# Attention heads: the order of score tiles, transposes and low parts on TensorE and VectorE

## The chip, the cores and the metric

The kernel runs on one core of one Trainium2 chip. The metric is the device time of one execution in microseconds (us); the figure for a kernel is the median of its runs.

## What is computed

Two sequences of 512 tokens with 1024 features go through a trunk of two layers: Fourier mixing and a squared-ReLU MLP, then grouped-query attention and a second MLP. The change touches the attention heads only. There are 8 query heads and 2 key/value heads of 128 features for each sequence, so 16 heads in all:

```python
q = axial_rope(rms_norm(q, q_gain)) * (HEAD_DIM ** -0.5)
k = axial_rope(rms_norm(k, k_gain))
s = jnp.einsum("bqkgd,bskd->bkgqs", q_blk, k)
p = jax.nn.softmax(s, axis=-1)
o = jnp.einsum("bkgqs,bskd->bqkgd", p, v)
```

Everything is in 32-bit floats. A product is made of three passes over operands that are split into a high part (rounded to the short format that TensorE takes at full rate) and a low part (the rest).

## The kernel before

The kernel is one straight program of Tile code: the instructions of each engine are ordered by a scheduler at compile time, except inside a `manual_schedule` block, where the named engines keep the order of the source. Every engine runs its own list in order and waits by semaphores.

One helper makes every three-pass product: `mm3`, lines 81 (high by high), 82 (the moving operand's low part) and 83 (the stationary operand's low part). `split` takes a tile apart: line 86 is a ScalarE cast that makes the high part, line 87 a VectorE subtraction that makes the low part. `behind(x, y)` tells the scheduler that x must stand after y on their engine.

The heads loop runs over n = 1 to 16. In turn n it makes the scores of head n and finishes head n - 1. These names are used below, all for one turn:

- **S0 to S3**, the four score tiles (`scores`, line 1510): 128 queries by 512 keys each, one `mm3` of three 512-column matmuls. After each: a row maximum on VectorE (line 1512), an exponential on ScalarE that also sums (line 1514, two records: the activation and the reading of the sum), a reciprocal on VectorE (line 1515) and a scaling on GpSimd (line 1516), which leaves the probabilities p0 to p3 of head n.
- **T0 to T3**, the transposes of head n - 1's probabilities (`transpose_p`, line 1522): four 128-column transposes each, one out of each of p0 to p3 of the turn before. Each is followed by a split out of PSUM: a cast (line 86) and a low part (line 87).
- **Q**, the transposes of head n + 1's query (`transpose_q`, line 1501), four of them, and a split.
- **V**, the product of the values with the transposed probabilities (`values`, line 1531): four `mm3` groups, one for each of T0 to T3, so twelve 512-column matmuls. The first matmul of group i takes the high part of Ti, the second its low part. After it a ScalarE copy (line 1538) and, for the eight heads of the first sequence, a split as well (line 1541).

In the source a turn is S0, T0, S1, T1, S2, T2, S3, T3, Q, V. No engine has a manual order in this loop: the scheduler sets it. Two other streams run through the loop. In turns 3 to 7 the last query rows are normalised and rotated (`todo`, lines 155 to 160, 1467, 1475, 1478, 1480). From turn 7 on the first weights of the output projection are loaded and split (`first_rows`; line 86 and 87 on tiles named w); the `fresh` lines put such a low part behind the last low part and the last reciprocal of a turn.

The PSUM pool has eight buffers of one bank, the pool of the probabilities eight tiles.

Of the kernel before, what the change touches and what calls it, by code (L numbers as in the profile page):

```python
# [16 lines left out]
ALU = mybir.AluOpType  # L17
AX = mybir.AxisListType
# [5 lines left out]
NT = S // P  # L24
# [20 lines left out]
def trunk_kernel(ctx, tc, x_in, xt_in, y_out, tables, rope, gfour, gcol, grow, gfin,  # L45
                 w_four, w_nyq, w_qkv, w_o, w_a22, w_up, w_row2, w_row4, w_sum2, w_sum4, w_down):
    nc = tc.nc
# [17 lines left out]
    def slot(shape, dt):  # L65
        return act.tile(shape, dt, tag="u4", name=nm("u"))

    def tm(shape=(P, 512), dt=F32):
        return tmp.tile(list(shape), dt, tag="t2", name=nm("t"))

    def small(n=4):
        return sm.tile([P, n], F32, tag="s", name=nm("s"), padded_shape=[P, 8])

    def ps():
        return psp.tile([P, 512], F32, tag="ps", name=nm("ps"))

    def f32(ap):
        return ap.bitcast(F32)

    def mm3(out, lh, ll, rh, rl, first, last):  # L80
        nc.tensor.matmul(out, lh, rh, start=first, stop=False)  # L81
        nc.tensor.matmul(out, lh, rl, start=False, stop=False)  # L82
        nc.tensor.matmul(out, ll, rh, start=False, stop=last)  # L83

    def split(dst_hi, dst_lo, src, eng=nc.vector):
        hi = nc.scalar.copy(dst_hi, src)  # L86
        return hi, eng.tensor_sub(dst_lo, src, f32(dst_hi))  # L87

    def behind(x, y, sync=False):

        kind = mybir.DependencyClass.Sync if sync else mybir.DependencyClass.NoSync
        tc.add_manual_dep(x.ins, y.ins.name, mybir.DependencyInfo(kind, mybir.DependencyReason.SCHED_ONLY),
                          reason="order")
# [5 lines left out]
    def load_raw(src, shape=(P, 1024)):  # L99
        raw = rawp.tile(list(shape), F32, tag="raw", name=nm("raw"))  # L100
        nc.sync.dma_start(raw, src)
        return raw
# [618 lines left out]
    ET = mybir.EngineType  # L721
# [714 lines left out]
    def head_squares(raw, h0, n, ss, scale=1.0):  # L1436
        junk = tm((P, n * HD), BF16)
        for h in range(h0, h0 + n):
            nc.scalar.activation(junk[:, (h - h0) * HD : (h - h0 + 1) * HD], raw[:, h * HD : (h + 1) * HD],
                                 AF.Square, scale=scale, accum_out=ss[:, h : h + 1])  # L1440
# [41 lines left out]
            yield  # L1482

    vt, kr, kT, qr = {}, {}, {}, {}
    heads_out, ahead, fresh, last_made = Blocks(None), [], [], []

    def transpose_k(q):
        for h in range(NKV):
# [8 lines left out]
    def transpose_q(q, h):  # L1497
        pt = ps()
        c = (h % 2) * HD
        for t in range(NT):  # L1500
            nc.tensor.transpose(pt[:, t * P : (t + 1) * P], qr[q, h // 2][:, t, c : c + HD], ident)  # L1501
        qT = slot([P, 2, 512], F32R)
        split(qT[:, 0], qT[:, 1], pt)
        return qT

    def scores(q, h, qT, t):
        kk = kT[q, h // 4]
        s = ps()
        cols = slice(t * P, (t + 1) * P)
        mm3(s, qT[:, 0, cols], qT[:, 1, cols], kk[:, 0], kk[:, 1], True, True)  # L1510
        m, sm_ = small(1), small(1)
        nc.vector.tensor_reduce(m[:, :1], s, AX.X, ALU.max, negate=True)
        p = tm()
        last_made[:] = [nc.scalar.activation(p, s, AF.Exp, bias=m[:, :1], accum_out=sm_[:, :1]),
                        nc.vector.reciprocal(sm_[:, :1], sm_[:, :1])]
        nc.gpsimd.tensor_scalar(p, p, sm_[:, :1], 1.0, ALU.mult, ALU.mult)
        return p

    def transpose_p(probs, sc):
        pt = ps()  # L1520
        for t in range(NT):
            nc.tensor.transpose(pt[:, t * P : (t + 1) * P], probs[t][:, sc * P : (sc + 1) * P], ident)  # L1522
        k = slot([P, 2, 512], F32R)
        return k, split(k[:, 0], k[:, 1], pt)

    def values(q, h, pts):
        o = ps()
        c = (h // 4) * HD
        for sc in range(NT):
            vh, vl = vt[q][0][:, sc, c : c + HD], vt[q][1][:, sc, c : c + HD]  # L1530
            mm3(o, vh, vl, pts[sc][:, 0], pts[sc][:, 1], sc == 0, sc == NT - 1)
        i, j = h // 2, h % 2
        name = "b11" if h < 4 else "b21"
        if j == 0:
# [99 lines left out]
    def tile_qkv(cg, q, t):  # L1634
        if (cg, q, t) in transposes:
            transpose_k(transposes[cg, q, t])
        if (cg, q) == (2, 0):
            o = qkv(cg, q, t, ws[cg], KC - 2, KC, begun[t])
        else:
            o = qkv(cg, q, t, ws[cg])  # L1640
        if (cg, q, t) == (2, 0, 0):
            token_scale(1)
        r = rs[q][:, t : t + 1]
        if cg == 2:
            split_scaled(vt[q][0][:, t], vt[q][1][:, t], o[:, 256:], r)
            return norm_rope(o, NKV, rt["k"], [t], [kr[q][:, t]], scale=r)
        outs = [qr[q, 2 * cg + i][:, t] for i in range(2)]
        if (cg, q, t) != (1, 1, 1):
            return norm_rope(o, 4, rt["q"], [t], outs, scale=r)
        raw = slot([P, 512], F32)  # L1650
        nc.scalar.activation(raw, o, AF.Copy, scale=r)
        return norm_rope(raw, 4, rt["q"], [t], outs)


    with tc.manual_schedule(engines={ET.Activation, ET.DVE}):
        for cg in (2, 0, 1):
            later = next_ws({2: 0, 0: 1}[cg]) if cg != 1 else iter(())
            for q in range(NSEQ):
# [26 lines left out]
    heads = [(q, h) for q in range(NSEQ) for h in range(NH)]  # L1685
    raw, ss = slot([P, 1024], F32), small(8)
    with tc.manual_schedule(engines={ET.Activation}):
        o = qkv(1, 1, 2, ws[1])
        tc.keep_in_program_order(nc.scalar.preload_act_table_set("natural_log_exp_and_others"))
        probs = [scores(*heads[0], first, t) for t in range(NT)]  # L1690
        nc.scalar.activation(raw[:, :512], o, AF.Copy, scale=rs[1][:, 2:3])
        qT = transpose_q(*heads[1])
        for _ in turned:
# [4 lines left out]
    todo = norm_rope(raw, 4, rt["q"], [2, 3], [qr[1, 2 + i][:, t] for t in (2, 3) for i in range(2)],  # L1698
                     ss, 2, nc.gpsimd)
    assert next(keeping, 0) == 0  # L1700
    first_rows = (None for _ in range(4) for _ in load_kept())
    for n in range(1, len(heads) + 1):
        pts, nxt = [], []
        for t in range(NT):
            if n < len(heads):
                nxt.append(scores(*heads[n], qT, t))
            k, both = transpose_p(probs, t)
            pts.append(k)
            if t == NT - 1 and fresh:
                for a, b, c in zip(fresh.pop(), both, last_made):  # L1710
                    behind(a, b)
                    if nxt:
                        behind(a, c)
            if n > 2 and t == 0:
                for _ in range(3 if n == 3 else 1):
                    next(todo, None)
        last = nxt[-1] if nxt else last
        if n + 1 < len(heads):
            qT = transpose_q(*heads[n + 1])
        values(*heads[n - 1], pts)  # L1720
        if n == 2:
            head_squares(raw, 4, 4, ss)
        probs = nxt
        if n > 6:
            next(first_rows, None)

    blocks = Blocks(2 * KC)
    behind(nc.scalar.activation(one[:, :1], last[:, :1], AF.Sqrt), both[0])
# [1 line left out]
    todo, e, rows = heads_out.plain_sums(), [tm() for _ in range(4)], []  # L1730
# [80 lines left out]
    for f in range(2 * PLAIN):  # L1811
        raw = load_raw(plain[f], (P, 2, 512))
# [60 lines left out]
    with tc.manual_schedule(engines={ET.PE, ET.Activation, ET.DVE, ET.Pool, ET.SP}):  # L1873
# [17 lines left out]
        x, z = xtok  # L1891
# [58 lines left out]
        for i in range(2):  # L1950
            a, b = slice(i * 256, i * 256 + 256), slice(512 + i * 256, 768 + i * 256)
# [158 lines left out]
```

## Time and profile before

| | |
|---|---|
| median of 3 runs | 1675.03 us (1674.89 to 1676.52) |
| the profiled execution's own time | 1675.69 us |
| its span, first to last instruction | 1673.9 us |
| PE busy | 1662.0 us (99%) |
| DVE (VectorE) busy | 1263.5 us (75%) |
| ACT (ScalarE) busy | 871.5 us (52%) |
| POOL (GpSimd) busy | 392.5 us (23%) |
| heads loop, first S0 to last V, by TensorE's rows | 843.06 to 964.64 us of the span |

In the rows of the profile PE is TensorE, PEld its weight loads, DVE VectorE, ACT ScalarE, POOL GpSimd. Matmuls are pipelined, so that a matmul's row is longer than the distance to the next one; what TensorE needs is read from the distance between starts. The same holds for DVE and ACT, whose records overlap a little when they stand back to back. A row of a timeline gives start, duration, engine, line, operation, output and input, the count of merged instructions, and in brackets the idle time before it and who ended it.

### The profile page before, as it was taken

The page shows a single profiled execution, that of the slowest core. Times are in us where ns is not written, and L with a number is a line of the kernel's source. Part 1 is how long each engine was busy: PE and PEld are TensorE (multiplying, and loading weights), DVE is VectorE, ACT ScalarE, POOL GpSimd, SP SyncE. Part 2 cuts the span into 40 slices and gives each one's busy share as a digit, 9 for nine tenths or more (in the row PEclk, how much of TensorE's full clock was granted, in tenths as well). Part 3 has the DMA queues.
Part 4 walks back from the last instruction along what each step waited for, and adds up shares of the span by engine and source line. Part 5 has one row for each costly group of instructions (what it writes and reads, how often), then busy time and mean ns, then how long its engine had stood idle before and what let it go on. Part 6 is the DMA issues. An engine that isn't in the chain of part 4 may idle for free.

```text
span 1673.9 us, 22285 instructions
## 1 busy us (share of the span) xinstructions
PE 1662.0 (99%) x7845; PEld 1387.2 (83%) x7845; DVE 1263.5 (75%) x1848; ACT 871.5 (52%) x1539; POOL 392.5 (23%) x364
## 2 busy tenths in 40 slices
PE   9999999999999999999999999999999999999998
PEld 8988888888888888888888888888888888888887
DVE  8879776557886869869888877777854487978865
ACT  6766444446342435447688855554554552433334
POOL 3321443221000001325454303004422220000002
PEclk9999999999999999999999999999999999999999
DMA  9843655449775757425501146334544696757522
GB/s 310 264 152 110 210 184 188 152 168 370 253 228 165 247 172 233 163 83 198 168 1 39 63 177 226 114 120 169 209 147 167 225 373 192 228 157 248 167 101 101
DMA packets 122321, 303.00 MB, mean 181 GB/s; under 512 B 12217, under 2 KB 13881, under 8 KB 122209
## 3 DMA queue, kind: packets, MB, share of 16 engines
q1 hardware_dynamic: 98848, 254.18, 43.8%
q0 software_dynamic: 8960, 21.05, 6.0%
q10 hardware_dynamic: 14400, 26.35, 4.2%
q8 instruction: 61, 1.00, 0.2%
q14 instruction: 52, 0.42, 0.1%
HBM read 218.11 MB, written 82.38 MB: 180 GB/s over the span
## 4 chain that ended last, share of the span: by engine, by line
PE 95%; DVE 2%; DMA 1%; ACT 1%; issue 1%; POOL 0%; SPq 0%; DVEq 0%; POOLq 0%; ACTq 0%
PE ps L927 74%; PE ps L83 6%; PE ps L81 6%; PE ps L82 6%; PE ps L1522 2%; DMA u<-x 0%; DMA u<-w_four 0%; PE ps L1501 0%; DMA raw<-w_up 0%; PE ps L191 0%; PE ps L496 0%; PE ps L493 0%; DVE w L87 0%; DVE u L715 0%; DVE raw L977 0%
## 5 line engine op out<-in xcount | busy, mean ns | idle before, releaser
L927 PE MATMUL ps<-u,w 128*128 128x512 f32 x4944 | 1131.0, 389 | 0.0
L927 PEld LDWEIGHTS ps<-u,w 128*128 128x128 f32 x4944 | 926.5, 188 | 194.9 <-ACT u L960 1.7
L86 ACT CAST w<-raw 128x1024 fp32r<-128x1024 f32 (+1 forms) x216 | 213.7, 994 | 308.4 <-PE ps L927 234.7
L87 DVE TENSOR_TENSOR w<-raw,w 128x1024 fp32r<-128x1024 f32 (+1 forms) x216 | 251.3, 1167 | 75.5 <-ACT w L86 75.3
L86 ACT CAST u<-u 128x1024 fp32r<-128x1024 f32 x144 | 145.0, 1047 | 87.0 <-PE ps L927 37.8
L87 DVE TENSOR_TENSOR u<-u,u 128x1024 fp32r<-128x1024 f32 x144 | 173.4, 1232 | 18.7 <-ACT u L86 17.8
L927 PE MATMUL ps<-u,u 128*128 128x512 f32 x600 | 143.2, 389 | 0.3 <-DVE t L1014 0.3
L1164 POOL DMA_DIRECT2D raw<-w_sum x32 | 27.7, 866 | 468.3 <-DMA raw<-w_sum 207.1
L1137 DVE TENSOR_TENSOR u<-ps,u 128x512 f32<-128x512 f32 x160 | 109.3, 685 | 37.1 <-PE ps L927 34.5
L1045 POOL TENSOR_TENSOR u<-u 128x512 f32<-128x512 f32 x28 | 37.6, 1343 | 425.0 <-ACT u L942 425.0
L927 PEld LDWEIGHTS ps<-u,u 128*128 128x128 f32 x600 | 112.5, 188 | 24.4 <-DVE t L1014 0.7
L81 PE MATMUL ps<-u,u 128*128 128x512 f32 (+2 forms) x340 | 128.7, 381 | 0.0
L83 PE MATMUL ps<-u,u 128*128 128x512 f32 (+2 forms) x340 | 124.0, 366 | 0.1
L82 PE MATMUL ps<-u,u 128*128 128x512 f32 (+2 forms) x340 | 123.6, 364 | 0.0
L182 POOL TENSOR_TENSOR t<-t,t 128x512 f32<-128x512 f32 (+1 forms) x54 | 79.3, 1472 | 188.1 <-ACT t L178 187.2
L941 ACT ACTIVATE t<-t 128x512 f32<-128x512 f32 x64 | 40.5, 632 | 109.9 <-DVE t L1014 96.4
L83 PEld LDWEIGHTS ps<-u,u 128*128 128x128 f32 x340 | 64.2, 189 | 11.0 <-DVE u L468 0.5
L87 DVE TENSOR_TENSOR u<-ps,u 128x512 fp32r<-128x512 f32 (+3 forms) x112 | 68.0, 634 | 5.5 <-ACT u L86 4.9
L82 PEld LDWEIGHTS ps<-u,u 128*128 128x128 f32 x340 | 64.4, 189 | 8.4 <-DVE u L87 0.3
L81 PEld LDWEIGHTS ps<-u,u 128*128 128x128 f32 x340 | 64.4, 189 | 7.8
L1001 DVE TENSOR_TENSOR t<-ps,u 128x512 f32<-128x512 f32 x32 | 22.0, 687 | 59.9 <-PE ps L927 52.0
L86 ACT CAST u<-ps 128x512 fp32r<-128x512 f32 (+3 forms) x112 | 59.4, 557 | 8.1 <-PE ps L1522 6.1
(266 smaller groups left out, 2012.4 us busy)
## 6 DMA issues: line engine op xcount, KB each, us to landing
raw<-w_up SPq DMA_DIRECT2D x80, 512.0 KB, 4.6
u<-spill_t SPq DMA_DIRECT2D x60, 512.0 KB, 6.9
raw<-w_sum SPq DMA_DIRECT2D x56, 512.0 KB, 5.8
u<-spill_b SPq DMA_DIRECT2D x45, 512.0 KB, 6.3
spill_t<-u SPq DMA_DIRECT2D x84, 256.0 KB, 2.0
spill_b<-t ACTq DMA_DIRECT2D x60, 256.0 KB, 4.4
raw<-w_row SPq DMA_DIRECT2D x28, 512.0 KB, 5.1
park<-u SPq DMA_DIRECT2D x24, 512.0 KB, 4.8
```

The lines of the kernel that those rows point to most:

```text
L81: nc.tensor.matmul(out, lh, rh, start=first, stop=False)
L82: nc.tensor.matmul(out, lh, rl, start=False, stop=False)
L83: nc.tensor.matmul(out, ll, rh, start=False, stop=last)
L86: hi = nc.scalar.copy(dst_hi, src)
L87: return hi, eng.tensor_sub(dst_lo, src, f32(dst_hi))
L182: nc.gpsimd.tensor_add(acc[q][:, :n], acc[q][:, :n], s[:, :n])
L927: nc.tensor.matmul(o, w[x][:, sl], h[k][y], start=first and k + i == 0, stop=k == n - 1 and i == 2, skip_group_check=not first)
L941: nc.scalar.activation(t, src, AF.Relu)
L1045: eng.tensor_sub(t[:, 0], b12, b11)
L1137: return nc.vector.tensor_add(x, o, x)
L1164: nc.gpsimd.dma_start(s[:, 1], w[:, 3], accum_op=ALU.add)
L1522: nc.tensor.transpose(pt[:, t * P : (t + 1) * P], probs[t][:, sc * P : (sc + 1) * P], ident)
```

## The change

The loop is put into a `manual_schedule` block for TensorE, so its order there is that of the source. The source order becomes S0, S1, T0, T1, Q, S2, S3, T2, T3, V: scores and transposes come in pairs, and Q follows T1 instead of T3. The maximum of S2 is put behind two low parts on VectorE, that of T1 and that of Q. The orders of VectorE, ScalarE and GpSimd are still the scheduler's. No instruction is added or removed.

```diff
     def transpose_q(q, h):
...
-        split(qT[:, 0], qT[:, 1], pt)
+        q_low[:] = split(qT[:, 0], qT[:, 1], pt)[1:]
         return qT
...
-        nc.vector.tensor_reduce(m[:, :1], s, AX.X, ALU.max, negate=True)
+        maxima.append(nc.vector.tensor_reduce(m[:, :1], s, AX.X, ALU.max, negate=True))
...
-    for n in range(1, len(heads) + 1):
-        pts, nxt = [], []
-        for t in range(NT):
-            if n < len(heads):
-                nxt.append(scores(*heads[n], qT, t))
-            k, both = transpose_p(probs, t)
-            pts.append(k)
...
-        if n + 1 < len(heads):
-            qT = transpose_q(*heads[n + 1])
-        values(*heads[n - 1], pts)
...
+    with tc.manual_schedule(engines={ET.PE}):
+        for n in range(1, len(heads) + 1):
+            pts, nxt = [], []
+            for t in range(NT):
+                if n < len(heads) and t % 2 == 0:
+                    nxt += [scores(*heads[n], qT, i) for i in range(t, t + 2)]
+                    if t:
+                        for x in (both[1], *q_low):
+                            behind(maxima[-2], x)
+                k, both = transpose_p(probs, t)
+                pts.append(k)
...
+                if t == 1 and n + 1 < len(heads):
+                    next_q = transpose_q(*heads[n + 1])
...
+            qT = next_q
+            values(*heads[n - 1], pts)
```

TensorE in turn 10, before, from S0's last matmul: in these rows ps_8681 is S0, ps_8692 T0, ps_8700 S1, ps_8711 T1, and t_8584 to t_8641 are the probabilities of the head before.

```order
L83 MATMUL ps_8681<-u_6950,u_8658 128x512
L1522 MATMUL ps_8692<-ident,t_8584 128x128
L1522 MATMUL ps_8692<-ident,t_8603 128x128
L1522 MATMUL ps_8692<-ident,t_8622 128x128
L1522 MATMUL ps_8692<-ident,t_8641 128x128
L81 MATMUL ps_8700<-u_6950,u_8658 128x512
```

TensorE in the same turn, with the change, from S1's last matmul: ps_8694 is S1, ps_8705 T0, ps_8713 T1, ps_8721 Q, ps_8729 S2.

```order
L83 MATMUL ps_8694<-u_6950,u_8622 128x512
L1522 MATMUL ps_8705<-ident,t_8586 128x128
L1522 MATMUL ps_8705<-ident,t_8597 128x128
L1522 MATMUL ps_8705<-ident,t_8632 128x128
L1522 MATMUL ps_8705<-ident,t_8643 128x128
L1522 MATMUL ps_8713<-ident,t_8586 128x128
L1522 MATMUL ps_8713<-ident,t_8597 128x128
L1522 MATMUL ps_8713<-ident,t_8632 128x128
L1522 MATMUL ps_8713<-ident,t_8643 128x128
L1501 MATMUL ps_8721<-ident,u_6944 128x128 x4
L81 MATMUL ps_8729<-u_6950,u_8622 128x512
```

Twelve transposes stand in one row where there were four between two score tiles, and Q, which stood directly ahead of V, now stands six matmuls and eight transposes ahead of it.

VectorE in turn 10, before, from S1's maximum on: L1512 are the maxima of S1, S2, S3; L87 the low parts of T1, T2, T3, Q and, last, of a weight tile (w); L1515 the reciprocals.

```order
L1512 TENSOR_REDUCE s_8704<-ps_8700 128x1
L1515 RECIPROCAL s_8686<-s_8686 128x1
L87 TENSOR_TENSOR u_8716<-ps_8711,u_8716 128x512
L1512 TENSOR_REDUCE s_8723<-ps_8719 128x1
L1515 RECIPROCAL s_8705<-s_8705 128x1
L87 TENSOR_TENSOR u_8735<-ps_8730,u_8735 128x512
L1512 TENSOR_REDUCE s_8742<-ps_8738 128x1
L1515 RECIPROCAL s_8724<-s_8724 128x1
L87 TENSOR_TENSOR u_8754<-ps_8749,u_8754 128x512
L87 TENSOR_TENSOR u_8762<-ps_8757,u_8762 128x512
L1515 RECIPROCAL s_8743<-s_8743 128x1
L87 TENSOR_TENSOR w_8473<-u_8472,w_8473 128x512
```

VectorE in the same turn, with the change, after the maxima of S0 and S1: the low parts of T0, T1 and Q (ps_8705, ps_8713, ps_8721), the maximum of S2 (ps_8729), the low part of T2, the maximum of S3 (ps_8740), the low part of T3 (ps_8759), and the weight tile's.

```order
L1515 RECIPROCAL s_8688<-s_8688 128x1
L87 TENSOR_TENSOR u_8710<-ps_8705,u_8710 128x512
L1515 RECIPROCAL s_8699<-s_8699 128x1
L87 TENSOR_TENSOR u_8718<-ps_8713,u_8718 128x512
L87 TENSOR_TENSOR u_8726<-ps_8721,u_8726 128x512
L1512 TENSOR_REDUCE s_8733<-ps_8729 128x1
L87 TENSOR_TENSOR u_8756<-ps_8751,u_8756 128x512
L1512 TENSOR_REDUCE s_8744<-ps_8740 128x1
L1515 RECIPROCAL s_8734<-s_8734 128x1
L87 TENSOR_TENSOR u_8764<-ps_8759,u_8764 128x512
L1515 RECIPROCAL s_8745<-s_8745 128x1
L87 TENSOR_TENSOR w_8475<-u_8474,w_8475 128x512
```

Before, Q's low part stands last of the five and the low parts of T2 and T3 each follow one maximum; now Q's stands third, and S2's maximum, T2's low part, S3's maximum and T3's low part all follow it.

ScalarE in the same turn, with the change: L1514 are the exponentials of S0, S1, S2 and S3, L86 the casts of T0, T1, Q, T2, T3 and of the weight tile, L1538 the copy out of V.

```order
L1514 ACTIVATE t_8690,s_8688<-ps_8683,s_8687 128x512
L86 CAST u_8710<-ps_8705 128x512
L1514 ACTIVATE t_8701,s_8699<-ps_8694,s_8698 128x512
L86 CAST u_8718<-ps_8713 128x512
L86 CAST u_8726<-ps_8721 128x512
L86 CAST u_8756<-ps_8751 128x512
L86 CAST u_8764<-ps_8759 128x512
L1514 ACTIVATE t_8736,s_8734<-ps_8729,s_8733 128x512
L1514 ACTIVATE t_8747,s_8745<-ps_8740,s_8744 128x512
L86 CAST w_8475<-u_8474 128x512
L1538 COPY u_8676<-ps_8767 128x512
```

Before, casts and exponentials alternate through the whole turn (T0, S0, T1, S1, T2, S2, T3, Q, S3); with the change the exponentials of S2 and S3 come after all five casts. In the turns of the first sequence the second and third row here change places (the cast of T1 stands ahead of the exponential of S1).

After the loop all engines' orders are the same as before.

More of the change, by code (lines that the diff above doesn't have):

```diff
@@ L1484, in trunk_kernel @@
     vt, kr, kT, qr = {}, {}, {}, {}
-    heads_out, ahead, fresh, last_made = Blocks(None), [], [], []
+    heads_out, ahead, fresh, last_made, maxima, q_low = Blocks(None), [], [], [], [], []
     def transpose_k(q):
@@ L1701, in trunk_kernel @@
     first_rows = (None for _ in range(4) for _ in load_kept())
-    for n in range(1, len(heads) + 1):
-        pts, nxt = [], []
-        for t in range(NT):
-            if n < len(heads):
-                nxt.append(scores(*heads[n], qT, t))
-            k, both = transpose_p(probs, t)
-            pts.append(k)
[L1709 to L1717, printed above, removed]
-        if n + 1 < len(heads):
-            qT = transpose_q(*heads[n + 1])
-        values(*heads[n - 1], pts)
[L1721 to L1725, printed above, removed]
+    with tc.manual_schedule(engines={ET.PE}):
[9 more added lines that the diff above has]
+                pts.append(k)
+                if t == NT - 1 and fresh:
+                    for a, b, c in zip(fresh.pop(), both, last_made):
+                        behind(a, b)
+                        if nxt:
+                            behind(a, c)
+                if t == 1 and n + 1 < len(heads):
+                    next_q = transpose_q(*heads[n + 1])
+                if n > 2 and t == 0:
+                    for _ in range(3 if n == 3 else 1):
+                        next(todo, None)
+            last = nxt[-1] if nxt else last
+            qT = next_q
+            values(*heads[n - 1], pts)
+            if n == 2:
+                head_squares(raw, 4, 4, ss)
+            probs = nxt
+            if n > 6:
+                next(first_rows, None)
     blocks = Blocks(2 * KC)
```

## The prediction

> **What bounds the kernel now.** I read the page's first part and its chain first, then TensorE's rows through the heads loop, then those of VectorE, ScalarE and GpSimd at the places where TensorE could wait for them.
>
> ```profile
> PE 1662.0 (99%) x7845; PEld 1387.2 (83%) x7845; DVE 1263.5 (75%) x1848; ACT 871.5 (52%) x1539; POOL 392.5 (23%) x364
> PE 95%; DVE 2%; DMA 1%; ACT 1%; issue 1%; POOL 0%; SPq 0%; DVEq 0%; POOLq 0%; ACTq 0%
> ```
>
> TensorE is busy for 99% of the span and makes 95% of the chain. The change takes no work from it, so it can gain only what TensorE waits for in the heads loop. The query transposes (Q) mark the turns; these are the first, the two around the longest turn, two in an undisturbed stretch, and the last of 14:
>
> ```profile
> 847.75 0.44 PE ps L1501 x4
> 863.23 0.44 PE ps L1501 x4
> 871.55 0.44 PE ps L1501 x4
> 933.89 0.44 PE ps L1501 x4
> 941.63 0.44 PE ps L1501 x4
> 949.37 0.44 PE ps L1501 x4
> ```
>
> 13 turns take 101.62 us, 7.82 each; an undisturbed one takes 7.74, the longest 8.32. What TensorE needs is in the distances between starts:
>
> ```profile
> 937.63 0.60 PE L1522 MATMUL ps<-ident,t 128*128 128x128 f32 x4
> 937.98 0.48 PE L81 MATMUL ps<-u,u 128*128 128x512 f32 x1
> 938.30 0.40 PE L82 MATMUL ps<-u,u 128*128 128x512 f32 x1
> 938.53 0.39 PE L83 MATMUL ps<-u,u 128*128 128x512 f32 x1
> 941.04 0.60 PE L1522 MATMUL ps<-ident,t 128*128 128x128 f32 x4
> 941.47 0.60 PE L1501 MATMUL ps<-ident,u 128*128 128x128 f32 x4
> 942.14 0.39 PE L82 MATMUL ps<-u,u 128*128 128x512 f32 x1
> ```
>
> A matmul takes 0.23 (938.30 to 938.53). Four transposes and a matmul take 0.67 (937.63 to 938.30), eight and a matmul 1.10 (941.04 to 942.14): 0.11 a transpose, whatever the length of the run. A turn of 24 matmuls and 20 transposes is 5.52 + 2.20 = 7.72. So an undisturbed turn is at the floor, and all that the 13 turns lose is 101.62 - 13 x 7.74 = 1.0 us.
>
> **The change, part by part.** Pairing by itself costs and gains nothing on TensorE: 0.11 a transpose in runs of four and of eight. What changes is when VectorE and ScalarE deliver. A timetable for that needs their steps, start to start:
>
> ```profile
> 938.26 0.59 ACT L86 CAST u<-ps 128x512 fp32r<-128x512 f32 x1 [0.53 <-PE ps L1522]
> 938.75 0.69 ACT L1514 ACTIVATE t<-ps,s 128x512 f32<-128x512 f32 x1
> 939.42 0.59 ACT L86 CAST u<-ps 128x512 fp32r<-128x512 f32 x1
> 940.26 0.69 ACT L1514 ACTIVATE t<-ps,s 128x512 f32<-128x512 f32 x1 [0.26 <-DVE s L1515]
> 938.88 0.69 DVE L87 TENSOR_TENSOR u<-ps,u 128x512 fp32r<-128x512 f32 x1 [0.29 <-ACT u L86]
> 939.49 0.68 DVE L1512 TENSOR_REDUCE s<-ps 128x1 f32<-128x512 f32 x1
> 940.09 0.15 DVE L1515 RECIPROCAL s<-s 128x1 f32<-128x1 f32 x1
> 940.16 0.67 DVE L87 TENSOR_TENSOR u<-ps,u 128x512 fp32r<-128x512 f32 x1
> 936.12 0.64 ACT L86 CAST w<-u 128x512 fp32r<-128x512 f32 x1
> 936.79 1.08 DVE L87 TENSOR_TENSOR w<-u,w 128x512 fp32r<-128x512 f32 x1 [0.32 <-ACT w L86]
> 898.57 0.39 PE L83 MATMUL ps<-u,u 128*128 128x512 f32 x1
> 899.00 0.69 DVE L1512 TENSOR_REDUCE s<-ps 128x1 f32<-128x512 f32 x1 [0.61 <-PE ps L83]
> 961.28 2.48 DVE L87 TENSOR_TENSOR u<-ps,u 128x512 fp32r<-128x512 f32 x4 [0.50 <-ACT u L86]
> 962.03 0.19 PEld L82 LDWEIGHTS ps<-u,u 128*128 128x128 f32 x1 [0.17 <-DVE u L87]
> ```
>
> - On ScalarE a cast holds the engine 0.48 (938.26 to 938.75), an exponential with the reading of its sum 0.67 (938.75 to 939.42).
> - On VectorE a maximum or a low part holds 0.60, a reciprocal 0.07 (940.09 to 940.16).
> - Maximum to its exponential, 0.77 (939.49 to 940.26); cast to its low part, 0.62 (938.26 to 938.88); for a weight tile 0.67, and its low part holds about 1.05.
> - A score tile's last matmul to its maximum, 0.43 (898.57 to 899.00). A low part's start to the matmul that takes it, 0.75 (961.28 to 962.03).
>
> VectorE keeps its order even where later work is ready: the reciprocal below waited 0.29 us for an exponential, and the two low parts behind it, whose casts had ended by 896.25, waited with it.
>
> ```profile
> 895.18 1.07 ACT L86 CAST u<-ps 128x512 fp32r<-128x512 f32 x2
> 896.13 0.72 ACT L1514 ACTIVATE t<-ps,s 128x512 f32<-128x512 f32 x1
> 896.97 0.16 DVE L1515 RECIPROCAL s<-s 128x1 f32<-128x1 f32 x1 [0.29 <-ACT t L1514]
> 897.05 1.27 DVE L87 TENSOR_TENSOR u<-ps,u 128x512 fp32r<-128x512 f32 x2
> ```
>
> So an exponential is 0.84 ahead of its reciprocal (896.13 to 896.97).
>
> *A turn of the first sequence, no other stream beside it.* Time 0 is S0's first matmul. TensorE's own places are S2 at 2.70, T2 at 4.08, V at 4.96, and V's second matmul on T3 at 4.96 + 10 x 0.23 = 7.26. The new orders give one chain: maximum of S0 at 0.46 + 0.43 = 0.89; its exponential 1.66; cast T0 2.33; cast T1 2.81; exponential of S1 3.29; cast Q 3.96; low part of Q 4.58; then, because the maximum of S2 stands behind it, that maximum at 5.18; low part of T2 5.78; maximum of S3 6.38; reciprocal; low part of T3 at 7.05. TensorE can take it at 7.80, 0.54 late. S2 and its maximum could have been done from 3.6 on: the new wait holds it, and behind it in VectorE's queue stand the low parts of T2 and T3, which V waits for. Before, T3's low part at 942.83 was usable at 943.58, while V (first matmul at 941.83) came to it at 944.13, 0.55 early:
>
> ```profile
> 941.83 0.47 PE L81 MATMUL ps<-u,u 128*128 128x512 f32 x1
> 942.83 0.67 DVE L87 TENSOR_TENSOR u<-ps,u 128x512 fp32r<-128x512 f32 x1
> ```
>
> This holds in turns 2 and 5 to 9: 6 x 0.54 = 3.2 us. Ten links, each known to about 0.03, give 0.3 to 0.8 a turn.
>
> *Turns 10 to 14, with a weight tile.* The exponential of S1 stands ahead of the cast of T1, so low parts come at 4.10 (T1) and 4.70 (Q), then the maximum of S2 5.30, T2's low part 5.90, maximum of S3 6.50, T3's low part 7.17. But VectorE's turn ends later still: exponential of S3 7.27, weight cast 7.94, weight low part 8.61 to 9.66. TensorE's next S0 has its maximum ready at 7.17 + 0.75 + 0.46 + 0.89 = 9.27, so VectorE is 0.39 late, and from then on VectorE's and ScalarE's loop sets the pace. From one maximum of S0 to the next: 0.77 + 0.67 + 0.48 + 0.67 + 0.62 to T1's low part, four steps of 0.60 to the maximum of S3, then 0.77 + 0.67 + 0.67 + 1.05: 8.77 us. Against 7.74 this is 1.0 a turn, 5 x 1.0 = 5.0 us. The lower bound is the 0.54 of the other turns (the weight tile hidden), the upper one 1.5, if the late exponentials hold up the next transposes as well. Turn 15 has no Q, one step less, and starts late: 0.9.
>
> *Turn 1.* Four squarings (line 1439) stand ahead of the first exponential in both kernels; it starts 0.29 later than in the chain above, and T2's low part is late as well: 0.9, bounds 0.4 to 1.3.
>
> ```profile
> 843.06 0.39 PE L81 MATMUL ps<-u,u 128*128 128x512 f32 x1
> 845.01 0.67 ACT L1514 ACTIVATE t<-ps,s 128x512 f32<-128x512 f32 x1
> ```
>
> *Turns 3 and 4.* In turn 3 the new order has T2's and T3's low parts, with the small steps of the rows' norm between, ahead of the maxima of S2 and S3, and three scalings (line 1467; two took 0.70) ahead of S2's exponential, V's copy between it and S3's.
>
> ```profile
> 862.99 0.70 ACT L1467 ACTIVATE u<-u,s 128x128 f32<-128x128 f32 x2 [0.26 <-DVE s L160]
> 897.23 0.69 POOL L1516 TENSOR_SCALAR t<-t,s 128x512 f32<-128x512 f32 x1 [0.87 <-DVE s L1515]
> ```
>
> By the steps above the maximum of S2 starts at 7.3 after T3's low part, its exponential behind the scalings at 8.3, S3's behind V's copy at 9.4 (7.15 in the chain above), its reciprocal at 10.3; GpSimd's scaling of p3 (0.26 to its start, 0.70 long) ends at 11.3. V of turn 3 is in time, but T0 of turn 4 has its fourth transpose at 9.5 and waits 1.9 for p3; with 0.3 of the usual wait behind it 2.2, bounds 1.0 to 3.0.
>
> Turn 16 has the order it had, and no row after the loop moves.
>
> Sum: 3.2 + 5.0 + 0.9 + 0.9 + 2.2 = 12.2 of new waits, less the 1.0 that the old order loses: +11.2 us. The profiled execution's own time is 1675.69 (span 1673.9 and 1.8 around it), so 1686.9; it lies 0.66 above the median of the runs, 1675.03, so the median comes to 1686.2. With all bounds low the sum is 1.8 + 2.7 + 0.5 + 0.4 + 1.0 - 1.0 = +5.4, with all high 4.8 + 7.5 + 1.3 + 1.3 + 3.0 - 1.0 = +16.9: 1680.4 to 1691.9.
>
> Twelve transposes in one run deserve a look at the clock:
>
> ```profile
> 959.72 2.22 PE L1522 MATMUL ps<-ident,t 128*128 128x128 f32 x16
> 958.00:966.00 8.00, 7.91 (x44) 6.44 (x43) 6.87 (x12) 6.78 (x13) 1.40 (x2) 1.00 0.01 3
> ```
>
> Sixteen in a row, 2 us of nothing else, ran at a granted clock of 1.00. The Trainium skill, page "TensorE: Matmul & The Clock Gate", section "Part 4: PE-mode transpose", says that transposes do not count as busy for the clock gate in the way matmuls do. By it, longer runs of transposes could lose the clock; the row above speaks against it.
>
> **The rivals.**
>
> 1. *The waits are hidden.* If the ten links of the chain were 0.05 shorter each, T3's low part would be in time, VectorE would catch up in its idle time, and TensorE would run at its floor: 1675.03 - 1.0 = 1674.0. For it: VectorE is busy only 75% of the span. Against it: every link is a measured distance, in this loop. Between this and the forecast, with the low part late in a few turns only, lies up to +3.3. Chance 0.16 for both.
> 2. *Faster: changing between matmuls and transposes costs TensorE something.* The first matmul after a run of transposes is 0.32 ahead of the next instead of 0.23 (937.98 to 938.30). If that 0.09 were lost at each change, three changes fewer in each of 15 turns would give 4.0, with the 1.0 of old waits 5.0: 1670.0. It decides only if the delivery also keeps up. Against it: the four transposes ahead take 0.09 less than their share, so nothing is lost. Chance 0.02.
> 3. *The lag feeds itself.* S2's and S3's exponentials late, so p2 and p3 late at GpSimd, so T0 of the next turn waits too, in every turn as I put it for turn 4: 15 x 1.9 - 1.0 = +27.5: 1702.5. Against it: in the chain above p3 is ready about 0.8 after the next S0 starts, and T0 stands at 1.38. Chance 0.07.
> 4. *The clock drops in the runs of transposes*: 12 x 0.11 = 1.32 us more in each of 15 turns on top of the forecast, +31: 1706. That would be the named rule at work; the clock row speaks against it. Chance 0.02.
>
> **How the numbers follow.** The forecast, new waits of 5 to 17 us, has the rest, 0.73. What a measurement of this kernel can tell from no change is about 0.2%, 3.3 us. Rival 1 lies within that, rival 2 beyond it on the fast side, all else is slower: faster 0.02, same 0.16, slower 0.82. The range takes the forecast's bounds and opens toward the partly hidden case below and toward rival 3 above: 1678 to 1694. About 0.2 is left out.
>
> **What the profile would show.** Right: TensorE's weight loads on line 82 wait for VectorE's line 87 once in nearly every turn, about half a microsecond; Q's distance is near 8.3 in turns 5 to 9 and near 8.8 in turns 10 to 14; the longest wait is at turn 4's first transposes, ended by GpSimd's line 1516; after the loop everything is shifted by one amount. Wrong: turns of 7.74 with no such waits (rival 1), distances under 0.11 a transpose (rival 2), waits for line 1516 in every turn (rival 3), a granted clock under 1 in the loop (rival 4).

## The result and the profile after

The changed kernel takes 1688.74 us (median of 6 runs, 1688.16 to 1689.74), the kernel before, run beside it, 1675.04 (1674.44 to 1676.52): a ratio of 1.008 with an interval of 1.007 to 1.0091. It is 13.7 us slower. The forecast was 1686.2, within 1678 to 1694. The profiled execution took 1688.65 (span 1686.9, 13.0 more than before).

The page of the changed kernel gives the busy times and the shares of the chain:

```profile
PE 1668.0 (99%) x7845; PEld 1386.8 (82%) x7845; DVE 1267.5 (75%) x1848; ACT 873.4 (52%) x1539; POOL 390.0 (23%) x364
PE 91%; DVE 5%; ACT 2%; DMA 1%; issue 1%; POOL 0%; SPq 0%; DVEq 0%; ACTq 0%; POOLq 0%
```

The work is the same. TensorE's share of the chain fell from 95% to 91%, and VectorE's rose from 2% to 5%. The view of the waits over the heads loop (836 to 985 us of the span) says where; its columns are who waited for whom, the sum in us, how often, and the longest:

```profile
PEld ps L82 <- DVE u L87: 17.4, 28, 0.8
ACT t L1514 <- DVE s L1512: 16.0, 26, 1.3
...
PEld ps L1522 <- POOL t L1516: 1.9, 3, 0.9
```

The matmul of line 82, which takes a low part, waits for line 87, which makes it: 28 times over the loop, so twice in nearly every turn (T2's and T3's), by up to 0.8 us. The second row is ScalarE's exponentials waiting for VectorE's maxima. A weight load's wait overlaps the matmuls ahead of it, so the price is read from the turns. These are starts of Q in the changed kernel: turns 1, 5, 6, 8, 9, 10, 11 and 14.

```profile
843.79 0.60 PE L1501 MATMUL ps<-ident,u 128*128 128x128 f32 x4
...
878.20 0.60 PE L1501 MATMUL ps<-ident,u 128*128 128x128 f32 x4
...
887.12 0.60 PE L1501 MATMUL ps<-ident,u 128*128 128x128 f32 x4
...
905.00 0.60 PE L1501 MATMUL ps<-ident,u 128*128 128x128 f32 x4
...
913.38 0.60 PE L1501 MATMUL ps<-ident,u 128*128 128x128 f32 x4
...
921.75 0.60 PE L1501 MATMUL ps<-ident,u 128*128 128x128 f32 x4
...
930.71 0.60 PE L1501 MATMUL ps<-ident,u 128*128 128x128 f32 x4
...
956.77 0.60 PE L1501 MATMUL ps<-ident,u 128*128 128x128 f32 x4
```

From turn 1 to turn 14 it is 112.98 us (956.77 - 843.79) where it was 101.62: +11.36. A turn of the quiet stretch takes 8.38 (905.00 to 913.38), turn 5 takes 8.92, turn 10 takes 8.96; none is at the 7.74 of before. From the last Q to the first row after the loop is 1.9 us longer than before once Q's earlier place (2.26: two score tiles and eight transposes) is taken off. The remaining differences, -1.5 ahead of the loop and +1.3 behind it, cancel; their cause is open (the same Q, last ahead of the loop, starts anywhere from 835.6 to 838.0 in the traces of this document).

The chain that the prediction worked out can be laid beside turn 8, where no other stream runs. These are the rows of the chain on VectorE and ScalarE, then the weight load of the matmul that takes T3's low part and the next turn's first matmul, in order of time; S0's first matmul starts at 902.74:

```profile
903.64 0.69 DVE L1512 TENSOR_REDUCE s<-ps 128x1 f32<-128x512 f32 x1 [1.13 <-PE ps L83]
...
904.42 0.69 ACT L1514 ACTIVATE t<-ps,s 128x512 f32<-128x512 f32 x1 [0.36 <-DVE s L1512]
...
905.11 1.06 ACT L86 CAST u<-ps 128x512 fp32r<-128x512 f32 x2
...
906.05 0.71 ACT L1514 ACTIVATE t<-ps,s 128x512 f32<-128x512 f32 x1
...
906.72 0.60 ACT L86 CAST u<-ps 128x512 fp32r<-128x512 f32 x1
...
907.35 0.69 DVE L87 TENSOR_TENSOR u<-ps,u 128x512 fp32r<-128x512 f32 x1 [0.28 <-ACT u L86]
...
907.96 0.68 DVE L1512 TENSOR_REDUCE s<-ps 128x1 f32<-128x512 f32 x1
...
908.56 0.68 DVE L87 TENSOR_TENSOR u<-ps,u 128x512 fp32r<-128x512 f32 x1
...
909.83 0.67 DVE L87 TENSOR_TENSOR u<-ps,u 128x512 fp32r<-128x512 f32 x1
...
910.55 0.19 PEld L82 LDWEIGHTS ps<-u,u 128*128 128x128 f32 x1 [0.72 <-DVE u L87]
...
911.11 0.40 PE L81 MATMUL ps<-u,u 128*128 128x512 f32 x1
```

| step, us from S0's first matmul | worked out | measured |
|---|---|---|
| exponential of S0 | 1.66 | 1.68 |
| exponential of S1 | 3.29 | 3.31 |
| low part of Q | 4.58 | 4.61 |
| maximum of S2 | 5.18 | 5.22 |
| low part of T2 | 5.78 | 5.82 |
| low part of T3 | 7.05 | 7.09 |
| weight load of the matmul that takes it | 7.80 | 7.81 |

The ten links held to 0.04 us. The turn is 8.37 long (902.74 to 911.11), not 7.80 + 0.46 = 8.26: the matmul that stood and the one behind it take 0.56 to the next score tile where two matmuls in flow take 0.46. That 0.1 per stand was left out of the forecast.

### The profile page after: what moved, and what is told of

Read it like the earlier page. It is cut to its first block, busy times and chain, and to the rows that moved or that the text cites. A ratio compares the mean times of both kernels' runs of the same rounds, so it can differ in the third digit from the quotient of the medians.

```text
span 1686.9 us, 22290 instructions
## 1 busy us (share of the span) xinstructions
PE 1668.0 (99%) x7845; PEld 1386.8 (82%) x7845; DVE 1267.5 (75%) x1848; ACT 873.4 (52%) x1539; POOL 390.0 (23%) x364
## 4 chain that ended last, share of the span: by engine, by line
PE 91%; DVE 5%; ACT 2%; DMA 1%; issue 1%; POOL 0%; SPq 0%; DVEq 0%; ACTq 0%; POOLq 0%
PE ps L927 73%; PE ps L82 5%; PE ps L83 5%; PE ps L81 5%; DVE u L87 2%; DVE s L1512 1%; ACT t L1514 1%; ACT u L86 1%; PE ps L1522 1%; DMA u<-x 0%; PE ps L191 0%; DMA raw<-w_sum 0%; PE ps L496 0%; DMA u<-spill_t 0%; PE ps L493 0%
## 5 line engine op out<-in xcount | busy, mean ns | idle before, releaser
L86 ACT CAST w<-raw 128x1024 fp32r<-128x1024 f32 (+1 forms) x216 | 213.8, 995 | 312.8 <-PE ps L927 242.2
L87 DVE TENSOR_TENSOR w<-raw,w 128x1024 fp32r<-128x1024 f32 (+1 forms) x216 | 251.3, 1167 | 75.5 <-ACT w L86 75.3
L86 ACT CAST u<-u 128x1024 fp32r<-128x1024 f32 x144 | 145.1, 1048 | 81.7 <-PE ps L927 31.7
L87 DVE TENSOR_TENSOR u<-u,u 128x1024 fp32r<-128x1024 f32 x144 | 173.4, 1232 | 17.6 <-ACT u L86 16.6
L82 PEld LDWEIGHTS ps<-u,u 128*128 128x128 f32 x340 | 64.2, 189 | 25.4 <-DVE u L87 17.4
L87 DVE TENSOR_TENSOR u<-ps,u 128x512 fp32r<-128x512 f32 (+3 forms) x112 | 69.0, 634 | 9.7 <-ACT u L86 9.1
L1516 POOL TENSOR_SCALAR t<-t,s 128x512 f32<-128x512 f32 x64 | 45.2, 707 | 86.5 <-DVE s L1515 59.7
```

## The experiments

All times below are medians over five rounds, each with its ratio to the kernel before on the same chip. "The 13 turns" are the starts of Q in turn 1 to turn 14, as above.

### The edge taken out

```diff
-                    if t:
-                        for x in (both[1], *q_low):
-                            behind(maxima[-2], x)
```

> Changed kernel without the edge loop: the maximum of S2 no longer has to stand behind the low parts of T1 and Q; TensorE's order is that of the changed kernel. Turns 4 to 7 keep the order of VectorE that they had (the scheduler chooses it there by itself); turns 1, 2 and 8 to 15 change: the maximum of S2 goes ahead of the low part of T1 and of Q, with the low part of Q still ahead of those of T2 and T3. Theory (VectorE's order delivers T2's and T3's low parts late): late by about 0.3 us in turns 8 and 9 and 0.4 in turns 10 to 14 instead of 0.6 and 0.95, so about 5 us less than the changed kernel, some 1683.5 us; the waits of line 82 for line 87 remain in turns 4 to 7. Rival A (the edge is the whole of it): about the kernel before, 1675. Rival B (the order on TensorE costs, whatever VectorE does): about the changed kernel, 1688.7.

Measured: 1684.44, ratio 1.0049 (1.0037 to 1.0062). First and last Q, and the waits for the low parts over the loop:

```profile
844.14 0.60 PE L1501 MATMUL ps<-ident,u 128*128 128x128 f32 x4
...
953.96 0.60 PE L1501 MATMUL ps<-ident,u 128*128 128x128 f32 x4
```

```profile
PEld ps L82 <- DVE u L87: 11.8, 18, 0.8
```

The 13 turns take 109.82, 3.2 less than with the edge. Turns 8 to 13 fell from between 8.37 and 8.96 to between 8.09 and 8.26; turns 3 to 7 did not move. So both one-cause rivals fall: the edge is about a third of the loss (3.2 of 11.4 by the turns; 39% by the ratios, 1.008 and 1.0049). ScalarE's order changed along with VectorE's: in turn 8 the exponential of S2 is back between the casts of T2 and T3, here and in the next run.

### TensorE's order kept, Q's low part last on VectorE

```diff
-                    if t:
-                        for x in (both[1], *q_low):
-                            behind(maxima[-2], x)
                 k, both = transpose_p(probs, t)
+                if t == NT - 1 and n + 1 < len(heads):
+                    behind(q_low[0], both[1])
```

> TensorE's order is exactly that of the changed kernel (pairs, Q's transposes with the first pair, written out). The edges on the maxima are gone, and one edge puts the low part of Q behind the low part of T3 instead, so that VectorE makes T0, T1, T2, T3's low parts and the four maxima first and Q's low part last. Theory (it is VectorE's order alone): the waits of line 82 for line 87 shrink to 0.1 to 0.3 us a turn, turns of about 7.8 to 8.1, the whole 1676 to 1680 us. Rival B (pairs and runs of twelve transposes cost TensorE something by themselves): about the changed kernel, 1688.7, with the waits gone but the distances longer.

Measured: 1679.89, ratio 1.0022 (1.0013 to 1.0031). First and last Q, and the same waits:

```profile
846.21 0.60 PE L1501 MATMUL ps<-ident,u 128*128 128x128 f32 x4
...
951.37 0.60 PE L1501 MATMUL ps<-ident,u 128*128 128x128 f32 x4
```

```profile
PEld ps L82 <- DVE u L87: 8.7, 21, 0.7
```

With TensorE's instructions in exactly the order of the changed kernel, 9.7 us of the loss are gone by the ratios (1.008 to 1.0022, of 1675), and the 13 turns take 105.16. Turns 8 to 13 are 7.78 to 7.89. What the changed kernel loses is thus mostly the order of VectorE, with that of ScalarE which the scheduler fits to it, and not the pairs or the runs of twelve transposes by themselves. Which of these two engines' orders counts for how much no run separates. Turns 5 to 7 are still at 8.32 to 8.34 (8.92 to 8.95 with the change).

### Pairs alone

```diff
...
+                    held = fresh.pop()
...
-                if t == 1 and n + 1 < len(heads):
+                if t == NT - 1 and n + 1 < len(heads):
                     next_q = transpose_q(*heads[n + 1])
+                    if held:
+                        for a, b in zip(held, q_low):
+                            behind(a, b)
```

The edge on the maxima is out here as well; `held` is the weight tile's cast and low part.

> Pairs alone: score tiles and transposes of the probabilities in pairs with TensorE's order written out, but Q's transposes stay behind the last pair as in the kernel before, no edge on the maxima, and the weight tile's cast and low part stand behind those of Q. Theory: pairing is free on TensorE (0.11 us a transpose in runs of four or eight), so about the kernel before, 1674 to 1676 us, with turns of 7.74 to 7.8. Rival B (pairs cost by themselves): several us above the kernel before.

Measured: 1678.45, ratio 1.0013 (1.0004 to 1.0022). First Q, that of turns 6 and 7, and the last:

```profile
847.97 0.60 PE L1501 MATMUL ps<-ident,u 128*128 128x128 f32 x4
...
888.35 0.60 PE L1501 MATMUL ps<-ident,u 128*128 128x128 f32 x4
...
896.67 0.60 PE L1501 MATMUL ps<-ident,u 128*128 128x128 f32 x4
...
951.45 0.60 PE L1501 MATMUL ps<-ident,u 128*128 128x128 f32 x4
```

Above the expected 1676 by 2.45, of which 1 is the chip (the kernel before took 1676.02 on it), and yet eight turns take 7.71 to 7.78, the floor. Pairs cost TensorE nothing there. The excess stands in turns 3 to 7, where the `todo` stream runs: 8.70 for turn 3 (8.32 before) and 8.32 (888.35 to 896.67) to 8.34 in turns 5 to 7 (7.89 before).

### TensorE's order written out alone

```diff
-                if n < len(heads) and t % 2 == 0:
-                    nxt += [scores(*heads[n], qT, i) for i in range(t, t + 2)]
-                    if t:
-                        for x in (both[1], *q_low):
-                            behind(maxima[-2], x)
+                if n < len(heads):
+                    nxt.append(scores(*heads[n], qT, t))
...
-                if t == 1 and n + 1 < len(heads):
+                if t == NT - 1 and n + 1 < len(heads):
```

> TensorE's order written out alone: single score tiles and transposes in the order of the kernel before, Q after T3, no edges. Theory: the scheduler's order of before was that order already, so within 0.5 us of the kernel before, 1674.5 to 1675.5. Rival C (the freedom of the scheduler hid waits, so writing the order out costs): 1 us or more above it, with new waits of line 82 or 1522 in the loop.

Measured: 1675.8, ratio 1.0002 (0.9993 to 1.001); the 13 turns take 102.30. Writing out the old order is free in the whole time, and costs 0.7 us by the turns: turn 3 is 8.79 where it was 8.32, turns 6 and 7 are 0.1 longer each. In the kernel before, the scheduler had left the order of the source in a few places, which the written-out order gives up: at the end of turn 3 the four pieces of the next T0 stand singly and in a pair among V's last and S0's matmuls (866.76 to 868.36), and later in the stretch of the `todo` stream matmuls of the next S0 stand between V's last ones.

### GpSimd's multiplication behind VectorE's

```diff
-            eng.tensor_mul(t1, x, every(table[:, 0, t]))
+            late = eng is nc.gpsimd
+            if not late:
+                eng.tensor_mul(t1, x, every(table[:, 0, t]))
             for b in range(2):
                 sl, other = slice(b * 64, b * 64 + 64), slice(64 - b * 64, 128 - b * 64)
-                nc.vector.tensor_mul(t2[:, :, sl], x[:, :, other], every(table[:, 1, t, sl]))
+                second = nc.vector.tensor_mul(t2[:, :, sl], x[:, :, other], every(table[:, 1, t, sl]))
+            if late:
+                behind(eng.tensor_mul(t1, x, every(table[:, 0, t])), second, True)
```

This is for the `todo` stream alone. In turn 5 of the changed kernel VectorE's two multiplications run beside GpSimd's:

```profile
879.45 1.08 DVE L1478 TENSOR_TENSOR t<-u,u 128x128 f32<-128x128 f32 x2
...
879.62 0.77 POOL L1475 TENSOR_TENSOR t<-u,u 128x256 f32<-128x256 f32 x1
```

> The changed kernel with one order turned round: GpSimd's multiplication of line 1475 waits for VectorE's two of line 1478 (turns 4 to 7) instead of running beside them. VectorE's and TensorE's orders are those of the changed kernel. Theory (beside GpSimd's multiplication the two of VectorE take 1.08 us instead of 0.48, and they stand ahead of T1's low part on the path): line 1478 back to 0.24 to 0.27 each, turns 5 to 7 from 8.93 to about 8.35, so 1.8 us less than the changed kernel, 1686.9 us. Rival (two more instructions ahead of T1's low part are the loss, wherever GpSimd stands): turns 5 to 7 stay at 8.9, 1688.7.

Measured: 1688.0, ratio 1.0073 (1.006 to 1.0086). The same two in turn 5 (lines 1480 and 1482 in this kernel), and Q of turns 1, 5, 6 and 14:

```profile
880.96 0.54 DVE L1480 TENSOR_TENSOR t<-u,u 128x128 f32<-128x128 f32 x2
...
881.65 0.74 POOL L1482 TENSOR_TENSOR t<-u,u 128x256 f32<-128x256 f32 x1 [0.49 <-DVE t L1480]
```

```profile
845.22 0.60 PE L1505 MATMUL ps<-ident,u 128*128 128x128 f32 x4
...
879.63 0.60 PE L1505 MATMUL ps<-ident,u 128*128 128x128 f32 x4
...
888.09 0.60 PE L1505 MATMUL ps<-ident,u 128*128 128x128 f32 x4
...
956.65 0.60 PE L1505 MATMUL ps<-ident,u 128*128 128x128 f32 x4
```

VectorE's pair takes half as long, 0.54, in the same place of an unchanged order of VectorE, ScalarE and TensorE. Turn 5 falls from 8.92 to 8.46, turns 6 and 7 from 8.93 and 8.95 to 8.36 and 8.39, and the 13 turns to 111.43: 1.55 less, against 1.8 expected. So two more instructions on the path cost next to nothing there, and their slowing is what costs. The whole times alone could not show it, since their intervals overlap. The Trainium skill, page "SBUF — State Buffer", section "Who interferes with whom", says that a VectorE instruction with two SBUF inputs contends with a GpSimd instruction that reads SBUF, because they share a port; the trace agrees that VectorE's pair is slowed beside GpSimd's, 1.08 us against 0.54 apart, and can't show the port.

The same edit on the kernel of pairs alone:

> The kernel of pairs alone (Q behind the last pair, no edge on the maxima) with the same turn of order: GpSimd's line 1475 waits for VectorE's line 1478. Theory: of what that kernel lost against the one before, all lies in turns 4 to 7; turns 5 to 7 go from 8.33 to about 7.75, which is 1.7 us less, 1676.7. Rival (line 1478 costs its place as well): no change, 1678.5. At best it would equal the kernel before; a gain of 1 us at most would need turn 4's distance of 8.7 to fall too.

Measured: 1676.31, ratio 1.0004 (0.9995 to 1.0013), and the 13 turns 102.24; turns 5 to 7 are at 7.92 to 7.98, above the expected 7.75. Of the 1.86 us by which the turns of pairs alone exceed those of before (103.48 against 101.62), the contention was 1.24. The 0.6 that is left is what writing the order out costs without pairs as well (102.30), with turn 3 at 8.69. Pairs, cleared of the contention, equal the old order written out; no version here beats the kernel before.

### TensorE's order left free

```diff
-    with tc.manual_schedule(engines={ET.PE}):
+    with nullcontext():
```

> The changed kernel with TensorE's order left to the scheduler, pairs and edges on the maxima as changed. The scheduler then puts the last matmuls of V, which wait for T3's low part, behind the first score tiles of the next query. Theory (the loss is TensorE standing at V for T2's and T3's low parts): TensorE has other work there, so most waits of line 82 go in turns 2 and 5 to 9, but in turns 10 to 14 the loop through VectorE and ScalarE still sets the pace: 1676 to 1683. Rival (the delivery itself is too slow in every turn, so that an order on TensorE can't help): 1686 to 1689.

Measured: 1681.77, ratio 1.0039 (1.0026 to 1.0051). The waits of its loop:

```profile
PEld ps L1522 <- POOL t L1516: 4.8, 12, 0.6
...
PEld ps L1522 <- ACT t L1514: 2.3, 5, 0.5
...
PEld ps L82 <- DVE u L87: 0.4, 2, 0.2
```

The scheduler puts next score tiles between V's matmuls, and the waits for low parts nearly vanish (17.4 to 0.4). Half the loss stays; the longest waits left on TensorE are those of the transposes for the probabilities (lines 1516 and 1514). So the written-out order makes the late low parts cost about 7 us more than they must. VectorE's and ScalarE's orders changed along with TensorE's in this run; what sets the rest was not taken further.

### Q early, without pairs

```diff
-                if n < len(heads) and t % 2 == 0:
-                    nxt += [scores(*heads[n], qT, i) for i in range(t, t + 2)]
-                    if t:
-                        for x in (both[1], *q_low):
-                            behind(maxima[-2], x)
+                if n < len(heads):
+                    nxt.append(scores(*heads[n], qT, t))
```

> No pairs and no edges: single score tiles and transposes as in the kernel before, TensorE's order written out, and only Q's transposes moved to stand behind T1. VectorE then has Q's low part ahead of T2's, but ScalarE and VectorE get work from the first score tile on without a gap. Theory (Q's low part and cast ahead of T2's and T3's make them late; one low part is 0.60 and the cast 0.48, against 0.55 of slack at V): 0.1 to 0.3 a turn over 14 turns, 1677 to 1680. Rival (Q's place alone makes the loss that is left without the edge): as the kernel without the edge, about 1684.

Measured: 1681.39, ratio 1.0034 (1.0022 to 1.0046): between the two expectations, so both missed. Turns 8 to 12 lose 0.1 to 0.2 each, as the theory had it, but turn 1 loses 0.8, and turns 3 and 4 take 9.92 and 9.35, 3.2 us more than before. The profiled execution is the slowest of the six, 1682.77. TensorE's rows show it stand twice at turn 4's T0 for GpSimd's scaling:

```profile
869.12 0.33 PE L1522 MATMUL ps<-ident,t 128*128 128x128 f32 x1 [0.92 <-POOL t L1516]
870.20 0.33 PE L1522 MATMUL ps<-ident,t 128*128 128x128 f32 x1 [0.75 <-POOL t L1516]
```

The windows around it (length; busy time and instructions of PE, PEld, DVE, ACT, POOL; the granted clock; the DMA share and GB/s) show something else behind that:

```profile
868.00:870.00 2.00, 0.53 (x2) 0.14 (x2) 1.26 (x4) 2.00 (x6) 1.24 (x2) 1.00 0.00 0
...
872.00:873.00 1.00, 1.00 (x5) 0.90 (x4) 1.00 (x2) 1.00 (x4) 0.55 (x1) 0.50 0.00 0
873.00:874.00 1.00, 1.00 (x4) 0.70 (x4) 0.40 (x3) 0.44 (x1) 0.61 (x1) 0.50 0.00 0
...
875.00:876.00 1.00, 1.00 (x8) 0.86 (x7) 0.80 (x2) 1.00 (x3) 0.00 (x0) 1.00 0.00 0
```

TensorE worked 0.53 us of 2, and a microsecond later its granted clock was halved for some 3.5 us, about 1.7 us of lost work. The Trainium skill, page "TensorE: Matmul & The Clock Gate", section "Part 1: The HAM clock gate (the "warmup" mystery)", has the clock halve after an idle window of about 3.4 us, whose start is not tied to the program; here a stretch of some 2.6 us without a score or values matmul (867.71 to 870.28) came ahead of it, which is shorter, so here the trace and the page differ. To see whether the stand was the cause, the norm's three steps that stand together in turn 3 were spread in this same kernel, with this edit on top of the one above:

```diff
-                    for _ in range(3 if n == 3 else 1):
+                    for _ in range(1):
```

> The kernel with single tiles and Q's transposes behind T1, with the three steps of the rows' norm that stand together in turn 3 made one a turn instead (the steps behind them move two turns on). That kernel lost 3.2 us of its 5.8 in turns 3 and 4, where TensorE stood for p3 and p4 behind the norm's steps and its granted clock then fell to 0.50 for 3.5 us. Theory (this loss is turn 3's steps, and the fall of the clock follows the stand): turns 3 and 4 of about 7.9, the clock 1.00 throughout, 1678 to 1679. Rival (single tiles with an early Q lose it in whichever turns the norm's steps stand): the same loss two turns later, about 1681.

Measured: 1680.02, ratio 1.0026 (1.0016 to 1.0036). Turns 3 and 4 take 7.98 and 7.85, and the granted clock stays at 1.00, as in this window of it:

```profile
870.00:880.00 10.00, 10.00 (x59) 8.24 (x59) 8.58 (x21) 8.52 (x21) 3.48 (x5) 1.00 0.01 2
```

That part of the theory held, in one profiled execution of each. But the whole gained only 1.4 by the medians, 2.1 by the two profiled executions (2.4 by their 13 turns), since the `todo` stream now lasts two turns longer and its turns 5 to 9 cost 8.2 to 8.6, 1.1 us more than without the spreading: a third of the loss by the turns, more by the medians, only moved, as the rival had it. Whether the clock fell in the other executions of the kernel without the spreading isn't known.

### Q's low part made twice

```diff
         q_low[:] = split(qT[:, 0], qT[:, 1], pt)[1:]
+        q_low[:] = [nc.vector.tensor_sub(qT[:, 1], pt, f32(qT[:, 0]))]
```

> The changed kernel with the low part of Q made twice on VectorE (the same subtraction into the same tile a second time; nothing else is added), the edge behind the second one. TensorE's order is that of the changed kernel. Theory (in every turn the path to T3's low part runs through VectorE's steps, and in turns 10 to 14 the whole loop does): one more step of 0.60 in each of turns 1 to 14, so about 8 us above the changed kernel, 1696 to 1697 (14 x 0.60 = 8.4). Rival (VectorE, idle for a fifth of a turn, takes it up in its gaps): less than 3 us above, 1689 to 1691.

Measured: 1696.42, ratio 1.0124 (1.0109 to 1.014).

```profile
844.39 0.60 PE L1501 MATMUL ps<-ident,u 128*128 128x128 f32 x4
...
964.81 0.60 PE L1501 MATMUL ps<-ident,u 128*128 128x128 f32 x4
```

The 13 turns take 120.42, 7.44 more than the changed kernel: 0.57 on average for each added step of 0.60. Single turns differ by -0.03 to 0.94, since the scheduler also moved other steps of VectorE and ScalarE, so the average is what can be read. In the changed kernel's window of the loop VectorE is busy for 122.48 of 149 us (third of the busy times), and still a step on this path costs nearly its whole length on average:

```profile
836.00:985.00 149.00, 141.53 (x749) 112.14 (x748) 122.48 (x244) 113.33 (x272) 54.19 (x76) 1.00 0.09 29
```

## Why the prediction was right

Right in its path and nearly right in size. By its own steps, each turn's length above 7.74:

| term | forecast | measured |
|---|---|---|
| turn 1 | 0.9 | 1.04 |
| turn 2 | 0.54 | 0.58 |
| turns 3 and 4 | 2.2 | 1.39 + 0.44 = 1.83 |
| turns 5 to 7 | 1.62 | 1.18 + 1.19 + 1.21 = 3.58 |
| turns 8 and 9 | 1.08 | 0.64 + 0.63 = 1.27 |
| turns 10 to 13 | 4.0 | 1.22 + 0.94 + 0.93 + 0.97 = 4.06 |
| turns 14 and 15 | 1.9 | 1.9, against before |
| old waits | -1.0 | -1.0 |
| sum | +11.2 | +13.3 |

- **The mis-sized term** is turns 5 to 7, which the prediction counted among those with "no other stream beside it". The two multiplications of line 1478 stand between T0's and T1's low parts there, on the path, and beside GpSimd's line 1475 they take 1.08. Putting GpSimd's multiplication behind VectorE's took 1.55 us back. This term is as large as the whole miss of about 2 us; the other terms' misses cancel. Without the slowing, turns 5 to 7 exceed 7.74 by 1.99, near the forecast 1.62 with 0.1 for each turn's stand. In the trace of before such a pair takes 0.48, with GpSimd's already done:

```profile
893.13 0.48 DVE L1478 TENSOR_TENSOR t<-u,u 128x128 f32<-128x128 f32 x2
```

- **The chain of ten links** was exact to 0.04. The 0.1 per stand that was left out shows in turns 8 and 9 (0.63 and 0.64 where 0.54 was forecast), less in turn 2 (0.58).
- **The weight tile's turns**: the loop through VectorE and ScalarE was put at 8.77, and turns 11 to 13 take 8.67 to 8.71; turn 10, on the way into it, 8.96.
- **Turn 4** waits at T0 for GpSimd's p3, as said, but for 1.0 us and not 1.9, and for p2 as well, 0.4. By the distances between starts these two stands are the 1.39 of the table. The maximum of S2 came 6.8 after turn 3's S0 (865.45 after 858.63) where 7.3 was forecast, and so p3 was done 10.7 after it and not 11.3. These are T0's first two pieces, its third, and its fourth with T1's four:

```profile
867.70 0.38 PE L1522 MATMUL ps<-ident,t 128*128 128x128 f32 x2
868.33 0.33 PE L1522 MATMUL ps<-ident,t 128*128 128x128 f32 x1 [0.26 <-POOL t L1516]
869.41 0.76 PE L1522 MATMUL ps<-ident,t 128*128 128x128 f32 x5 [0.76 <-POOL t L1516]
```

- **"The new wait holds it"** was half an answer. The prediction's chain named the maximum behind Q's low part as what delays T3. The runs split it: by the ratios, without the edge 5.2 us return, with Q's low part last as well another 4.5, with Q's transposes back behind T3 1.5, and without the contention 1.5 more. By the 13 turns, one profiled execution of each, these are 3.2, 4.7, 1.7 and 1.2 of the 11.4, with 0.6 left. Q's low part ahead of T2's and T3's costs about as much as the edge by the ratios, and more by the turns.
- **The rivals.** The waits were not hidden. Turns changing between matmuls and transposes less often gained nothing (pairs alone: 7.71 to 7.78 a turn). The lag did not feed itself: line 1516 held TensorE's weight loads in three places only. The clock did not drop: 1.00 over the loop.
- **The signs** came as said, but for two: the waits of line 82 came twice a turn and not once, and of turns 5 to 9 only 8 and 9 are near 8.3, with 5 to 7 near 8.9. The longest wait of the weight loads on lines 82 and 1522 is the one at turn 4's T0 (0.9).

## What to carry to other kernels

Where TensorE is at its floor, what decides is in which order the engines that feed it make what it takes next: a step of 0.6 us that is not needed until the next turn (Q's low part) costs much of its length when it stands ahead of one that is needed now, although that engine idles for a fifth of the loop: put last, it gave 0.36 a turn back, and made twice, it cost 0.57 a turn more. Before a chain is summed, look at every instruction of other streams that the new order leaves between its links, and at what runs beside it on an engine that can slow it. Compare distances between equal marks within a loop: they show 0.05 us a turn where whole times show 1 us.

## What the hardware showed that was not expected

- VectorE's multiplication of two 128x128 tiles takes 0.27 us alone, and a pair of them 1.08 instead of 0.47 to 0.54 beside GpSimd's 128x256 multiplication, which itself only goes from 0.74 to 0.77.
- The granted TensorE clock fell to 0.50 for some 3.5 us after about 2.3 us in which TensorE did little (867.95 to 870.20, two transposes), in one execution. In the changed kernel a similar stretch, 867.70 to 870.37 without a score or values matmul and busy for 0.99 us of two, left it at 1.00; what separates the two was not tried:

```profile
868.00:870.00 2.00, 0.99 (x7) 0.73 (x7) 1.46 (x5) 1.75 (x6) 1.61 (x3) 1.00 0.00 0
```

- A matmul that has stood for its low part takes 0.1 us more to the next than one in flow (the 0.56 against 0.46 of turn 8).
